# The row factors of the long sequence multiplied onto x by GpSimd, and the scale per feature put into the split of x

## The chip, the cores and the metric

The kernel runs on one core of a Trainium2 chip. The metric is the device time of one execution in microseconds (us); lower is better. Three runs of the kernel before the change took 2688.34, 2689.30 and 2693.07 us, a median of 2689.3 us.

A core has a matrix engine (TensorE, PE in the profile; loading its stationary operand is shown apart as PEld), three engines for elementwise work, which are VectorE (DVE), ScalarE (ACT) and GpSimd (POOL), and a queue that only starts DMAs (SyncE, SP). Each engine works through its own instructions strictly in order; an instruction that waits for another engine holds up all that stand behind it on its own engine.

## The reference

An encoder layer is applied to two sequences, a short one of 1024 rows (`x_prompt`) and a long one of 2048 rows (`x_sample`); 16 learned meta rows stand ahead of each. Cut to what matters here:

```python
def _rmsnorm(x, g):
    xf = x.astype(jnp.float32)
    y = xf * lax.rsqrt(jnp.mean(xf * xf, axis=-1, keepdims=True) + EPS)
    return (y * g.astype(jnp.float32)).astype(x.dtype)

def _encoder_layer(h, g_pre, w_in, b_in, ...):
    xn = _rmsnorm(h, g_pre)
    proj = xn @ w_in + b_in
    na_q, na_k, na_v, na_z, ml_qk, ml_v, ml_z, ml_o, ml_g, mg = jnp.split(proj, SPLIT_IDX, axis=-1)
    ya = neighbourhood_attention(na_q, na_k, na_v, na_rpb) * silu(na_z) @ w_a
    yb = mlstm_branch(ml_qk, ml_v, ml_g, ml_o, ...) * silu(ml_z) @ w_b
    ga, gb = jnp.split(jax.nn.sigmoid(mg), 2, axis=-1)
    return h + _rmsnorm((ga * ya + gb * yb) @ w_out, g_post)
```

The change concerns the first two lines of the layer: `xn = x * r * g_pre`, where `r` is one number per row (the inverse root of its mean square) and `g_pre` one number per feature.

## The kernel before

**The matrix products.** Operands are float32. To keep float32's precision TensorE is given each operand as a sum of a rounded part and a remainder, `x = xh + xl`, `w = wh + wl`, and every product is three matmuls: `xh*wh`, `xl*wh`, `xh*wl` (lines 217 to 219 in `mm3`, 786 to 788 in `tm_unit`). `xh` is made by ScalarE (a copy into the rounded type), `xl` by VectorE (x minus `xh`).

**Tiles and stages.** x lies transposed in SBUF, features on the 128 partitions: 1024 features are eight feature tiles k = 0 to 7, and a half of 512 rows is worked on at a time. `PLAN` is the list of column groups: `(0, 0, "m")`, `(0, 0, "nv")` for the short sequence, then `(1, 0, "mv")` and `(1, 1024, "mv")` for the two 1024-row pieces of the long one, then later groups that read x back from DRAM. `group` runs one of these: jobs of four columns, each first for the half 0 of the rows (`hf = 0`), then for half 1. Each column of a half is 24 matmuls of 128x512 (8 feature tiles times 3), and k goes up inside a column.

**Where the changed code runs.** `build_half(s, t0, res)` makes `xh` and `xl` of one half. For the long sequence (its last branch, lines 520 to 545) it runs four times: for rows 0, 512, 1024 and 1536, called builds 1 to 4 below. Each loads the rows (`tokens`), takes their squares on ScalarE and their factors on VectorE (`rsum`), spreads the factors over all partitions by a matmul with ones (`rrows`, result `rx`, one row of 512 factors on every partition), multiplies `xt` in place by `rx` and by `g_pre` (line 533, eight instructions of VectorE, one per feature tile), then splits it (line 540 ScalarE, line 541 VectorE, four of each, two feature tiles at a time). Builds 1 and 3 run beside the last job of the group before and must be done when the next group starts; builds 2 and 4 run beside `hf = 0` of their group's first job and must be done when `hf = 1` of that job starts. The halves `xh`, `xl` have two buffers each, so builds 3 and 4 also wait until TensorE has left the buffer. `xsplit` (lines 392 to 399) is the split that the short sequence uses: it takes one feature tile at a time and multiplies by the scale per feature on the way.

**What runs beside it.** The generator `sparse` issues the mLSTM scan and the neighbourhood attention between the matmuls of the dense groups. During builds 1 to 3 it is the mLSTM of the short sequence: TensorE multiplies a chunk's keys (`kth`, `ktl`, the split of the transposed keys, lines 1567 and 1568) and a chunk's scores (`sh`, `sl`, split by lines 1707 and 1713) between the columns' matmuls. Its small operands are made by ScalarE and VectorE, so these engines' work and the builds' work share two queues.

**What sets the order.** TensorE's instructions stand in the order in which the program issues them. The order on VectorE, ScalarE, GpSimd and SyncE is made by a scheduler at build time, which estimates each instruction's time; so moving a multiply from one engine to another also moves its neighbours. GpSimd's own work here is starting DMAs (lines 586, 604, 845, 677, 1107 and others) and a few memsets.

Of the kernel before, what the change touches and what calls it, by code (L numbers as in the profile page):

```python
# [10 lines left out]
F32 = mybir.dt.float32  # L11
F32R = mybir.dt.float32r
I32 = mybir.dt.int32
AF = mybir.ActivationFunctionType
ALU = mybir.AluOpType
# [122 lines left out]
class K:  # L138
# [337 lines left out]
    def build_half(self, s, t0, res):  # L476

        nc, wp = self.nc, self.wp
        if (s, t0) in self.xkept:
            assert not self.xput  # L480
            yield
            yield "scaled"
            x = []
            for name, part in zip(("xh", "xl"), self.xkept[s, t0]):
                x.append(wp.tile([P, KT, HALF], F32R, name=name, bufs=2))
                for k in range(0, KT, 4):
                    nc.sync.dma_start(x[-1][:, k:k + 4, :512].bitcast(F32), part[:, k:k + 4, :])
                yield
            res.append(tuple(x))
            return  # L490
        if s == 0:
            xts = self.xnext
            self.xnext = None
            while self.rwait:
                yield "wait"
            self.early = False
            yield "scaled"
            g = self.gpre
            p = self.psum("sm", [P, 512])
            nc.tensor.matmul(p[:, :KT], self.ident, g, start=True, stop=True)  # L500
            g = self.cp.tile([P, KT], F32, name="gx")
            nc.vector.tensor_copy(g, p[:, :KT])
            x, r = self.xparts(), []
            for e in range(4):
                self.xsplit(x, xts[e], e, 0, g)
                self.wflush(2)
                yield
            res.append(tuple(x))
            yield from self.rsum(self.toks, r)
            nc.vector.tensor_copy(self.rc[:, 4:8], r[0])  # L510
            dg = self.rdiag(r[0], self.toks[0][0])

            def rows():
                self.rrows(dg, self.rr[:, 1], "sm")
                self.xp.close()
                self.wside = self.wprep()
                self.sides.append([self.wside, 3])
            self.rwait[s, t0] = rows
        else:
            bp = self.bp  # L520
            toks, r = self.tokens(s, t0, range(4), bp, 4), []
            yield
            yield from self.rsum(toks, r)
            dg = self.rdiag(r[0], wp.tile([P, HALF], F32, name="st", bufs=4))
            xts = [self.xtload(s, t0, e, bp, 4) for e in range(4)]
            yield
            rr = bp.tile([P, 512], F32, name="rx", tag="thT", bufs=1)
            self.rrows(dg, rr, "pj")
            self.loose = False
            yield  # L530
            for k in range(KT):
                v = xts[k // 2][:, k % 2]
                nc.vector.scalar_tensor_tensor(v, v, self.gpre[:, k:k + 1], rr, op0=ALU.mult, op1=ALU.mult)
                if k % 2:
                    yield
            yield "scaled"
            x = self.xparts()
            for e in range(4):
                h = x[0][:, 2 * e:2 * e + 2, :512]
                nc.scalar.activation(h, xts[e], AF.Copy)  # L540
                nc.vector.tensor_tensor(x[1][:, 2 * e:2 * e + 2, :512], xts[e], h.bitcast(F32), op=ALU.subtract)
                yield
            res.append(tuple(x))
            self.loose = True
            self.xkeep(s, t0, x)
# [1651 lines left out]
```

## Time and profile before

| | |
|---|---|
| median of three runs | 2689.3 us |
| the profiled execution, its own time | 2690.81 us |
| the profiled execution, its span on the core | 2688.8 us |
| TensorE matmuls busy | 2641.9 us, 98% of the span |
| VectorE busy | 1942.2 us, 72% |
| ScalarE busy | 1440.3 us, 54% |
| GpSimd busy | 195.5 us, 7% |
| mean granted clock of TensorE | 0.995 |

The span is what the engines' records cover; the time measured around it is 2.0 us longer. TensorE is busy nearly all of the span, so the rows to look for are those in which it sat idle, and which engine ended that idleness. A row of the waits view reads: engine, line and tile that waited, arrow, what it waited for, then microseconds in total, times, and the longest. A row of a timeline reads: start, duration, engine, line, operation, output and inputs, and in brackets the idle time before it and what released it.

### The profile page before, as it was taken

How to read it: one execution, taken by the hardware profiler on the slowest of the kernel's cores; microseconds unless marked ns; L12 is line 12 of the kernel's file. 1: busy time of each engine (PE TensorE's matmuls, PEld its weight loads, DVE VectorE, ACT ScalarE, POOL GpSimd, SP SyncE). 2: the span in 40 equal slices, each digit the busy share in tenths (PEclk: the TensorE clock that was granted, in tenths of full speed). 3: DMA queues.
4: the chain of work that ended last, by engine and by line, in shares of the span. 5: the costliest groups of instructions: out<-in, count | busy, mean ns of one | idle time of the engine just before them, and what ended most of it. 6: DMA issues, size and time to landing. Idle time of an engine off the chain costs nothing.

```text
span 2688.8 us, 47086 instructions
## 1 busy us (share of the span) xinstructions
PE 2641.9 (98%) x15928; PEld 2331.0 (87%) x15928; DVE 1942.2 (72%) x5262; ACT 1440.3 (54%) x3388; POOL 195.5 (7%) x418
## 2 busy tenths in 40 slices
PE   9999999999999899999999999999999999999998
PEld 7898897899888899887888888887889898989888
DVE  5655678788667777546686776867478989898954
ACT  5423555554446555546665666656365656656521
POOL 0111130011301114000000000000000000000000
PEclk9999999999999999999999999999999999999999
DMA  9899988798867998989889998899899899998965
GB/s 377 323 332 338 329 288 318 269 347 304 299 222 248 364 352 295 317 270 282 261 273 337 360 301 265 277 348 324 273 324 308 257 300 286 279 310 257 327 241 202
DMA packets 394880, 805.73 MB, mean 300 GB/s; under 512 B 50608, under 2 KB 173440, under 8 KB 390800
## 3 DMA queue, kind: packets, MB, share of 16 engines
q1 hardware_dynamic: 363088, 702.49, 77.9%
q0 software_dynamic: 31552, 100.25, 10.1%
q8 instruction: 126, 2.06, 0.3%
q14 instruction: 114, 0.93, 0.1%
HBM read 548.96 MB, written 253.60 MB: 298 GB/s over the span
## 4 chain that ended last, share of the span: by engine, by line
PE 85%; DMA 8%; DVE 4%; ACT 2%; issue 1%; SPq 0%; DVEq 0%; ACTq 0%
PE pj L217 9%; PE pj L219 9%; PE pj L218 9%; PE pj L982 7%; PE pj L984 7%; PE pj L983 7%; PE pj L786 5%; PE pj L788 5%; PE pj L787 5%; PE pj L1944 3%; PE pj L1943 3%; PE pj L1945 3%; PE sm L1277 2%; DMA whl<-w 2%; PE tr L1262 2%; DMA stk<-nq 1%
## 5 line engine op out<-in xcount | busy, mean ns | idle before, releaser
L217 PE MATMUL pj<-xh,whl 128*128 128x512 f32 (+1 forms) x960 | 369.7, 385 | 2.7 <-DMA whl<-w 1.6
L219 PE MATMUL pj<-xh,whl 128*128 128x512 f32 (+1 forms) x960 | 360.9, 376 | 0.0
L218 PE MATMUL pj<-xl,whl 128*128 128x512 f32 (+1 forms) x960 | 360.2, 375 | 0.4 <-DVE xl L445 0.4
L786 PE MATMUL pj<-whl,xh 128*128 128x256 f32 (+1 forms) x1152 | 330.7, 287 | 10.5 <-DMA whl<-w 10.2
L788 PE MATMUL pj<-whl,xl 128*128 128x256 f32 (+1 forms) x1152 | 326.4, 283 | 0.0
L787 PE MATMUL pj<-whl,xh 128*128 128x256 f32 (+1 forms) x1152 | 326.1, 283 | 0.0
L786 PEld LDWEIGHTS pj<-whl,xh 128*128 128x128 f32 x1152 | 218.4, 190 | 11.5 <-DMA whl<-w 10.6
L1943 PE MATMUL pj<-whl,mh 128*128 128x256 f32 x768 | 218.3, 284 | 0.9 <-DMA whl<-w 0.9
L787 PEld LDWEIGHTS pj<-whl,xh 128*128 128x128 f32 x1152 | 218.3, 190 | 0.2
L788 PEld LDWEIGHTS pj<-whl,xl 128*128 128x128 f32 x1152 | 218.3, 189 | 0.0
L1944 PE MATMUL pj<-whl,mh 128*128 128x256 f32 x768 | 216.3, 282 | 0.0
L1945 PE MATMUL pj<-whl,mlo 128*128 128x256 f32 x768 | 215.4, 281 | 0.0
L219 PEld LDWEIGHTS pj<-xh,whl 128*128 128x128 f32 x960 | 181.2, 189 | 35.1
L217 PEld LDWEIGHTS pj<-xh,whl 128*128 128x128 f32 x960 | 181.2, 189 | 35.0 <-DMA whl<-w 2.0
L982 PE MATMUL pj<-xh,whl 128*128 128x512 f32 x512 | 206.9, 404 | 2.9 <-DMA xh<-t01h 1.5
L218 PEld LDWEIGHTS pj<-xl,whl 128*128 128x128 f32 x960 | 181.7, 189 | 30.5 <-issue 1.0
L984 PE MATMUL pj<-xh,whl 128*128 128x512 f32 x512 | 202.1, 395 | 0.0
L983 PE MATMUL pj<-xl,whl 128*128 128x512 f32 x512 | 201.0, 393 | 0.0
L1264 ACT ACTIVATE pts<-tr 96x384 fp32r<-96x384 f32 (+2 forms) x192 | 103.7, 540 | 109.2 <-PE tr L1262 108.5
L1269 DVE TENSOR_TENSOR pts<-tr,pts 96x384 fp32r<-96x384 f32 (+2 forms) x192 | 118.6, 618 | 53.5 <-ACT pts L1264 51.4
L217 PE MATMUL pj<-yh,whl 128*128 128x512 f32 x384 | 154.1, 401 | 0.0
L218 PE MATMUL pj<-yl,whl 128*128 128x512 f32 x384 | 151.5, 394 | 0.7 <-DVE yl L1845 0.7
(380 smaller groups left out, 6871.7 us busy)
## 6 DMA issues: line engine op xcount, KB each, us to landing
whl<-w SPq DMA_DIRECT2D x136, 1024.0 KB
whl<-q SPq DMA_DIRECT2D x112, 512.0 KB
w<-whl SPq DMA_DIRECT2D x36, 1024.0 KB
wraw<-wu SPq DMA_DIRECT2D x48, 512.0 KB
gt<-st SPq DMA_DIRECT2D x96, 256.0 KB
tg<-gt SPq DMA_DIRECT2D x96, 256.0 KB
q<-po POOLq DMA_DIRECT2D x26, 512.0 KB, 6.7
xt<-xt SPq DMA_DIRECT2D x24, 512.0 KB
```

The source lines that it names most:

```text
L217: mm(out, ah, bh, start=start, stop=False)
L218: mm(out, ah, bl, start=False, stop=False)
L219: mm(out, al, bh, start=False, stop=stop)
L786: nc.tensor.matmul(o, xh, wh, start=k == 0, stop=False)
L787: nc.tensor.matmul(o, xh, wl, start=False, stop=False)
L788: nc.tensor.matmul(o, xl, wh, start=False, stop=k == KT - 1)
L982: mm(bank, w[:, 0, k], xh[:, k], start=fresh and k == 0, stop=False, skip_group_check=True)
L983: mm(bank, w[:, 0, k], xl[:, k], start=False, stop=False, skip_group_check=True)
L984: mm(bank, w[:, 1, k], xh[:, k], start=False, stop=k == 3, skip_group_check=True)
L1943: nc.tensor.matmul(o, mh[:, k, xs], wh, start=clear > 0 and k == 0, stop=False)
L1944: nc.tensor.matmul(o, mh[:, k, xs], wl, start=False, stop=False)
L1945: nc.tensor.matmul(o, ml[:, k, xs], wh, start=False, stop=clear < 2 and k == KT - 1)
```

## The change

Two things change in `build_half`, in the branch for the long sequence. The eight multiplies by the row factors are now GpSimd's and no longer carry `g_pre`. The split is `xsplit`'s: eight instructions of 128x512 on ScalarE and eight on VectorE, each with `g_pre` as a scale per partition, in place of four and four of 128x1024. What is computed is the same up to rounding.

```diff
             for k in range(KT):
                 v = xts[k // 2][:, k % 2]
-                nc.vector.scalar_tensor_tensor(v, v, self.gpre[:, k:k + 1], rr, op0=ALU.mult, op1=ALU.mult)
+                nc.gpsimd.tensor_tensor(v, v, rr, op=ALU.mult)
                 if k % 2:
                     yield
             yield "scaled"
             x = self.xparts()
             for e in range(4):
-                h = x[0][:, 2 * e:2 * e + 2, :512]
-                nc.scalar.activation(h, xts[e], AF.Copy)
-                nc.vector.tensor_tensor(x[1][:, 2 * e:2 * e + 2, :512], xts[e], h.bitcast(F32), op=ALU.subtract)
+                self.xsplit(x, xts[e], e, 0, self.gpre)
                 yield
```

```python
    def xsplit(self, x, xt, e, base, gpre):
        nc = self.nc
        for k in (2 * e, 2 * e + 1):
            g, v = gpre[:, k:k + 1], xt[:, k % 2]
            h = x[0][:, k, base:base + v.shape[1]]
            nc.scalar.activation(h, v, AF.Copy, scale=g)
            nc.vector.scalar_tensor_tensor(x[1][:, k, base:base + v.shape[1]], v, g, h.bitcast(F32), op0=ALU.mult, op1=ALU.subtract)
```

Lines behind 541 stand two lower in the changed kernel: `ktl`'s line 1568 is 1566 there, `sl`'s line 1713 is 1711.

TensorE's instructions stand in the same order in both kernels. On the other engines the order changes at these places.

**GpSimd, builds 1 and 2.** `q` and `po` are DMAs of prepared weights, `raw`, `ss` and `st` small memsets for the mLSTM and the row factors. Before:

```order
L604 DMA q_4219<-po 128x1024
L604 DMA q_4221<-po 128x1024
L604 DMA q_4564<-po 128x1024
L358 MEMSET ss 128x5
L1426 MEMSET raw 128x1
L1584 MEMSET st 128x130
L1426 MEMSET raw 128x1
L604 DMA q11s_5750<-po 128x1024
```

and in the changed kernel:

```order
L602 DMA q_4219<-po 128x1024
L602 DMA q_4221<-po 128x1024
L533 ISA
L533 TENSOR_TENSOR xt<-xt,rx 128x512 x8
L602 DMA q_4564<-po 128x1024
L1424 MEMSET raw 128x1
L358 MEMSET ss 128x5
L1582 MEMSET st 128x130
L533 TENSOR_TENSOR xt<-xt,rx 128x512 x8
L1424 MEMSET raw 128x1
```

Eight multiplies stand in one piece in each build. Ahead of the first stands one instruction, ISA, that was not there before; the built program names it a reload of the library that holds GpSimd's operations.

**VectorE, build 1**, up to the second `ktl`, the remainder of the transposed keys. `vwl` and `st` belong to the mLSTM, `po` and `pr` to the prepared weights, `pj` is a column's result in PSUM. Before:

```order
L533 SCALAR_TENSOR_TENSOR xt<-xt,gpre,rx 128x512 x3
L1568 TENSOR_TENSOR ktl<-tr,kth 128x256
L533 SCALAR_TENSOR_TENSOR xt<-xt,gpre,rx 128x512 x3
L1439 SCALAR_TENSOR_TENSOR cv<-raw,cw,cv 128x16
L696 TENSOR_TENSOR pj<-pj,rr 128x512
...
L541 TENSOR_TENSOR xl<-xt,xh 128x2x512
L591 TENSOR_TENSOR pr<-pr 128x512
L1595 SCALAR_TENSOR_TENSOR st<-st,g_fb_3128,sm 128x130
L541 TENSOR_TENSOR xl<-xt,xh 128x2x512 x2
L1568 TENSOR_TENSOR ktl<-tr,kth 128x256
```

and in the changed kernel:

```order
L1566 TENSOR_TENSOR ktl<-tr,kth 128x256
L1437 SCALAR_TENSOR_TENSOR cv<-raw,cw,cv 128x16 x2
L694 TENSOR_TENSOR pj<-pj,rr 128x512
...
L1539 SCALAR_TENSOR_TENSOR vwl<-va_2774,g_wT_3114,vwh 128x130
L399 SCALAR_TENSOR_TENSOR xl<-xt,gpre,xh 128x512 x4
L694 TENSOR_TENSOR pj<-pj,rr 128x512
L399 SCALAR_TENSOR_TENSOR xl<-xt,gpre,xh 128x512 x2
L1566 TENSOR_TENSOR ktl<-tr,kth 128x256
```

No multiply stands ahead of the first `ktl` any more; ahead of the second stand six of the new split, where three of the old one stood.

**VectorE, build 2**, up to `sl`, the remainder of the second scores; `um`, `s` and `kl` belong to the mLSTM chunk. Before:

```order
L533 SCALAR_TENSOR_TENSOR xt<-xt,gpre,rx 128x512 x8
L1439 SCALAR_TENSOR_TENSOR cv<-raw,cw,cv 128x256
L541 TENSOR_TENSOR xl<-xt,xh 128x2x512 x3
...
L541 TENSOR_TENSOR xl<-xt,xh 128x2x512
L1656 TENSOR_TENSOR kl<-kf,kh 128x256
...
L1706 TENSOR_TENSOR um<-um,s_5623 128x256 x2
L1733 TENSOR_TENSOR num<-sm,num 128x128
L1713 TENSOR_TENSOR sl<-um,sh 128x256 x2
```

and in the changed kernel:

```order
L399 SCALAR_TENSOR_TENSOR xl<-xt,gpre,xh 128x512 x2
L1654 TENSOR_TENSOR kl<-kf,kh 128x256
L399 SCALAR_TENSOR_TENSOR xl<-xt,gpre,xh 128x512
L1699 TENSOR_TENSOR s_5637<-sc,s_5637 128x256
L399 SCALAR_TENSOR_TENSOR xl<-xt,gpre,xh 128x512
L1704 TENSOR_TENSOR um<-um,s_5637 128x256 x2
L1730 TENSOR_TENSOR num<-sm,num 128x260
L399 SCALAR_TENSOR_TENSOR xl<-xt,gpre,xh 128x512
L1711 TENSOR_TENSOR sl<-um,sh 128x256
L1731 TENSOR_TENSOR num<-sm,num 128x128
L1711 TENSOR_TENSOR sl<-um,sh 128x256
```

The last split of the build stood ahead of `kl`; now three splits stand between `kl` and `sl`, each waiting for ScalarE and through it for one of GpSimd's multiplies. In builds 3 and 4 GpSimd's sixteen multiplies stand in one row, ahead of the DMAs that open the neighbourhood attention (line 1107).

## The prediction

> **What bounds the kernel now.** I read the page's busy times first, then the chain that ended last, then what TensorE waited for.
>
> ```profile
> span 2688.8 us, 47086 instructions
> PE 2641.9 (98%) x15928; PEld 2331.0 (87%) x15928; DVE 1942.2 (72%) x5262; ACT 1440.3 (54%) x3388; POOL 195.5 (7%) x418
> PE 85%; DMA 8%; DVE 4%; ACT 2%; issue 1%; SPq 0%; DVEq 0%; ACTq 0%
> PE pj L786 <- DMA whl<-w: 10.2, 2, 7.6
> PE sm L219 <- DVE ktl L1568: 5.9, 5, 2.6
> ```
>
> TensorE is the bound, and its matmuls stay as they are, in number and order. So the change can move the time only through the microseconds in which TensorE stands still: it can remove some, or add some where a build's operands or the mLSTM's come later. The waits of the last row are the only ones near the builds that VectorE causes, and two of the five lie inside build 1:
>
> ```profile
> 430.97 0.38 PE L219 MATMUL sm<-vwh,ktl 128*128 128x260 f32 x1 [1.23 <-DVE ktl L1568]
> 437.32 0.28 PE L217 MATMUL sm<-vwh,kth 128*128 128x260 f32 x1
> 440.37 0.59 PE L219 MATMUL sm<-vwh,ktl 128*128 128x260 f32 x1 [2.64 <-DVE ktl L1568]
> 420.00:442.00 22.00, 18.13 (x85) 14.83 (x84) 21.19 (x52) 13.71 (x29) 0.76 (x2) 0.95 0.60 204
> 472.00:489.00 17.00, 17.00 (x83) 13.92 (x82) 14.41 (x25) 10.46 (x21) 0.10 (x1) 1.00 0.33 112
> 745.00:757.00 12.00, 12.00 (x60) 9.97 (x59) 10.21 (x41) 6.00 (x14) 0.55 (x1) 1.00 0.24 78
> 789.00:804.00 15.00, 15.00 (x68) 12.22 (x67) 14.08 (x17) 6.28 (x8) 0.00 (x0) 1.00 0.70 207
> ```
>
> The last four rows are the windows of builds 1 to 4; after the length come the busy times of PE, PEld, DVE, ACT and POOL. VectorE is full in build 1 (21.19 of 22 us) and nearly so in the others, GpSimd empty (0.00 to 0.76 us). That speaks for the move, as long as GpSimd does its part in time and does not slow VectorE.
>
> **The change part by part.** *VectorE and ScalarE.* Rows of the removed instructions, and of the same split where the kernel already uses it:
>
> ```profile
> L533 DVE SCALAR_TENSOR_TENSOR xt<-xt,gpre,rx x32: 717/748/754, 425.7 to 795.2; 128x512 f32<-128x512 f32 x32
> L541 DVE TENSOR_TENSOR xl<-xt,xh x16: 1218/1225/1229, 435.6 to 801.5; 128x1024 fp32r<-128x1024 f32 x16
> L540 ACT ACTIVATE xh<-xt x16: 1044/1050/1067, 433.1 to 798.7; 128x1024 fp32r<-128x1024 f32 x16
> L399 DVE SCALAR_TENSOR_TENSOR xl<-xt,gx,xh x8: 742/746/751, 32.4 to 37.4; 128x512 fp32r<-128x512 f32 x8
> L398 ACT ACTIVATE xh<-xt,gx x8: 727/732/741, 31.6 to 35.9; 128x512 fp32r<-128x512 f32 x8
> ```
>
> Per build VectorE loses 8 x 0.748 + 4 x 1.225 = 10.9 us and gains 8 x 0.746 = 6.0: 4.9 us less. ScalarE gets 8 x 0.732 - 4 x 1.050 = 1.7 us more, covered by its idle 8.3 us of 22 in build 1.
>
> *GpSimd's multiply, p.* The trace has no two-operand instruction of GpSimd. Its nearest rows:
>
> ```profile
> L1584 POOL MEMSET st<- 128x130 f32 x8 | 1.7, 210 | 97.0 <-DVE ccl L1685 92.3 <-DMA raw<-mq 4.7
> L358 POOL MEMSET ss<- 128x5 f32 x6 | 0.6, 103 | 76.0 <-DVE nwt L165 76.0
> L728 POOL COPY km<-st 128x16 f32<-128x16 f32 x4 | 0.9, 228 | 0.0
> ```
>
> The memsets give (210 - 103) / 125 = 0.86 ns per element on a fixed 0.10 us. One pass over 512 elements is 0.54 us, the floor; two passes (one per operand, the write beside them) are 0.98, three 1.42. The copy, if all of its 228 ns above 0.10 were per element, would give 8 ns each and 4.2 us, the ceiling; 16 elements are mostly fixed cost, so I stay with the memsets' slope and take 1.2, midway between two passes and three.
>
> *Spacing, q.* Whether GpSimd's two-operand instruction runs beside one of VectorE's with two operands in SBUF, the trace cannot show, since GpSimd has none. Ends: q = p = 1.2, they do not disturb each other; or they take turns, and each multiply is followed by one split, q = 1.2 + 0.75 = 1.95. I take turns as the likelier: both read the same memory at the same time, VectorE's queue is full in these windows, and nothing in the rows shows two such streams at once. The Trainium skill, page "SBUF — State Buffer", section "Who interferes with whom", says that VectorE with two SBUF inputs and a GpSimd instruction that reads SBUF exclude each other for a whole instruction; no run here shows it so far, and by it the sum would be the one below, without it that of the first rival.
>
> *The reload ahead of the first multiply.* Its place is behind the two DMA starts at 419.06 (over at 420.23). Nothing in the trace prices it: at least nothing, at most GpSimd's slowest transfer under this load, 10.7 us; I take the other row, 6.7 us, so that the first multiply starts at 426.9.
>
> ```profile
> 419.06 1.17 POOL L604 DMA_DIRECT2D q<-po  x2 [12.38 <-DVE st L378]
> q<-po POOLq DMA_DIRECT2D x26, 512.0 KB, 6.7
> pr<-wu POOLq DMA_DIRECT2D x16, 512.0 KB, 10.7
> ```
>
> The Trainium skill, page "GPSIMD Engine Reference", section "2.1 Instruction dispatch", puts the first call into freshly loaded code at about 6 us; this estimate would bring the start 0.7 us forward.
>
> *Build 1.* The first `ktl` no longer has multiplies ahead of it, so the wait of 1.23 goes. The second stands behind six splits: sixth multiply done at 426.9 + 6q, then ScalarE 0.73, VectorE 0.75 and `ktl` itself 0.42, 1.9 in all.
>
> ```profile
> 439.90 0.42 DVE L1568 TENSOR_TENSOR ktl<-tr,kth 128x256 fp32r<-128x256 f32 x1
> 462.87 0.50 PE L217 MATMUL pj<-xh,whl 128*128 128x512 f32 x1 [1.61 <-DMA whl<-w]
> ```
>
> Taking turns: 426.9 + 11.7 + 1.9 = 440.5, against 440.37 now: **+0.1**, the wait of 1.23 given back in a longer second one. The whole build has time until the group starts at 462.87, so its own result is not late.
>
> *Build 2.* The factors are ready at 473.44; TensorE wants `sl` at 488.45.
>
> ```profile
> 472.84 0.60 ACT L385 ACTIVATE rx<-pj 128x512 f32<-128x512 f32 x1 [0.49 <-PE pj L384]
> 486.36 0.76 DVE L1713 TENSOR_TENSOR sl<-um,sh 128x256 fp32r<-128x256 f32 x2
> 488.45 0.28 PE L219 MATMUL sm<-v,sl 128*128 128x130 f32 x1
> ```
>
> Now `sl` ends at 487.1, 1.3 us early. In the new order it follows the eighth split: 473.44 + 8q + 0.73 + 0.75, and 1.0 for the two `sl` and `num` between them. With q = 1.95 that is 491.5: **+3.0**. Queued behind these splits on VectorE are `um`, `num`, `sl`, on ScalarE `sh` and a column's evacuation; the first to be missed is `sl`.
>
> *Build 3.* The multiplies start at 745.67 and no split waits for the last of them, as ScalarE makes `xh` behind the evacuation at 753.64 anyway. But GpSimd works beside the mLSTM's chain on VectorE:
>
> ```profile
> 745.08 0.59 ACT L385 ACTIVATE rx<-pj 128x512 f32<-128x512 f32 x1
> 753.64 0.69 ACT L708 ACTIVATE st<-pj,bfm 128x512 f32<-128x512 f32 x1 [0.68 <-PE pj L219]
> 751.69 0.76 DVE L1706 TENSOR_TENSOR um<-um,s 128x256 f32<-128x256 f32 x2
> 753.05 0.42 DVE L1713 TENSOR_TENSOR sl<-um,sh 128x256 fp32r<-128x256 f32 x1
> 753.97 0.28 PE L219 MATMUL sm<-v,sl 128*128 128x130 f32 x1
> ```
>
> Taking turns, the two `um` and two `sl`, each with both inputs in SBUF, wait for one multiply each: 4 x 1.2 = 4.8, less the 0.5 between the end of `sl` and TensorE's wish: **+4.3**. Without disturbance 0: VectorE has 1.4 us less ahead of them.
>
> *Build 4.* Start 789.85 (ScalarE's `rx` at 789.25), no mLSTM beside it. TensorE takes feature tile k = 7 from 808.25 (the row is the first of its three matmuls in build 4's first column):
>
> ```profile
> 789.25 0.60 ACT L385 ACTIVATE rx<-pj 128x512 f32<-128x512 f32 x1 [2.37 <-PE pj L384]
> 808.25 0.40 PE L217 MATMUL pj<-xh,whl 128*128 128x512 f32 x1
> 751.08 0.55 POOL L1107 DMA_DIRECT2D qB<-onehot  x1 [22.41 <-PE sc L1694]
> 772.87 1.02 POOL L1194 DMA_DIRECT2D kx<-masks  x2
> 824.36 0.29 PE L1231 MATMUL sc<-kx,qB 128*128 128x288 f32 x1
> DMA to landing us min/median/max: 7.0/7.6/8.2
> ```
>
> Taking turns, the eighth split ends at 789.85 + 15.6 + 1.5 = 806.9: **0**, with 1.3 to spare. GpSimd's DMAs that open the attention stand behind these multiplies and move from 751 to 773 to about 806; their first use is the matmul at 824.36, and the masks' landing takes 8.2 us at most (last row), so that is covered.
>
> *Sum:* 0.1 + 3.0 + 4.3 + 0 = +7.4 us on the profiled execution's 2690.8, or 2698.2; its time lies 1.5 above the median of the runs, so the forecast is **2697 us** as a median (2689.3 + 7.4 = 2696.7). With p = 0.98 the builds give -1.2, +1.3, +3.4, 0: +3.5; with p = 1.42 they give +1.4, +4.8, +5.2 and +0.4: +11.8. A reload of 10.7 adds up to 4.0. Own range 2692 to 2704.
>
> **The rivals.** *No disturbance* (the engines run side by side, q = 1.2). Build 1's sixth multiply is done at 434.1, `ktl` at 436.0, when TensorE arrives (437.32 less the 1.23); both waits shrink, though the chain of ScalarE ahead of `kth` keeps about 0.9: -3.0. Builds 2 to 4 meet their times (485.5 for `sl`, against 488.45). 2689.3 - 3.0 = 2686 us, within 0.2%: not slower. For it: GpSimd is idle and VectorE gets 4.9 us back per build. Against it: it needs two engines to stream 512 elements from two operands each without one delaying the other.
>
> *A dear multiply* (p of 4.2 as the copy row could mean, decisive from about 2.1, where build 4's last tile passes 808.25). Then, even without turns, build 1 gives 426.9 + 25.2 + 1.9 - 440.4 = +13.6, build 2 473.4 + 33.6 + 2.5 - 488.4 = +21.1, build 4 789.85 + 33.6 + 1.5 - 808.25 = +16.7, together 51: 2740 us. The slope of the memsets speaks against it.
>
> *Luck of the order.* The scheduler also swaps loads on SP further on; TensorE's wait of 7.6 us for a weight load (first block) is of that kind. If it vanished in addition to build 1's two waits: 2689.3 - 3.0 - 7.6 = 2679 us. Nothing in the order says that it does.
>
> **How the numbers follow.** Taking turns 0.55, no disturbance 0.30, dear multiply 0.07, luck 0.08. 0.2% is 5.4 us, about what a measurement of this kernel tells from no change, so the borders are 2683.9 and 2694.7. A sixth of the first case (p near two passes) falls inside them: 0.09. Slower 0.46 + 0.07 = 0.53, same 0.30 + 0.09 = 0.39, faster 0.08. The range must hold both middle cases, of both signs: 2685 to 2706; the likeliest's own is the 2692 to 2704 above.
>
> **What would show it.** Right: multiplies of GpSimd of 1.0 to 1.4 us start to start alone, nearer 2 beside VectorE; VectorE's `um` and `sl` longer or later in build 3; a wait of TensorE for `sl` or `sh` of about 3 us near 488 and of about 4 near 754. Wrong: multiplies at an even 1.2 with VectorE's rows unchanged, no idle TensorE in builds 2 and 3, and one or none for `ktl` near 440. A first multiply later than 431 would mean a dearer reload; a wait in a column's matmuls near 808 a dearer multiply.

## The result, and the profile after

The changed kernel takes **2706.6 us** in the median of four runs (2702.6 to 2710.8), the kernel before 2691.2 (2688.3 to 2694.0): **1.0056 times as long, 95% interval 1.0045 to 1.0068**, about 15 us slower. The forecast was 2697 us, with a range of 2685 to 2706. The profiled execution took 2710.75 us, 1.8 of them around its span of 2709.0; it is the slowest of the four, so a time read from it is a few us too long for the median.

The page after, its span and busy times:

```profile
span 2709.0 us, 47121 instructions
PE 2652.7 (98%) x15928; PEld 2340.1 (86%) x15928; DVE 1950.8 (72%) x5246; ACT 1444.2 (53%) x3404; POOL 241.5 (9%) x450
```

TensorE has the same 15928 matmuls, yet it is *busy* 10.8 us longer (2641.9 before). VectorE has 16 instructions fewer and should be 20 us less busy; it is 8.6 us busier. Two things have become longer that the change does not touch. The first shows in VectorE's timeline in build 1. A row has the start, the duration and the instruction. In the kernel before:

```profile
421.12 0.16 DVE L166 SCALAR_TENSOR_TENSOR nwy<-nwt,nwy 128x4 f32<-128x4 f32 x1
422.31 0.16 DVE L166 SCALAR_TENSOR_TENSOR nwy<-nwt,nwy 128x4 f32<-128x4 f32 x1
423.65 1.11 DVE L1819 TENSOR_SCALAR hb<-hb,mv,nwy 128x128 f32<-128x128 f32 x4
```

and in the changed kernel, beside GpSimd's eight multiplies, which run from 420.78 to 430.80 (beyond line 540 its line numbers are two lower):

```profile
420.76 0.15 DVE L165 TENSOR_TENSOR nwt<-nwt,mv 128x4 f32<-128x4 f32 x1
420.95 1.15 DVE L166 SCALAR_TENSOR_TENSOR nwy<-nwt,nwy 128x4 f32<-128x4 f32 x1
422.14 1.22 DVE L164 SCALAR_TENSOR_TENSOR nwt<-nwy 128x4 f32<-128x4 f32 x1
...
428.38 1.22 DVE L166 SCALAR_TENSOR_TENSOR nwy<-nwt,nwy 128x4 f32<-128x4 f32 x1
429.52 0.69 DVE L694 TENSOR_TENSOR pj<-pj,rr 128x512 f32<-128x512 f32 x1
```

These are the steps of the inverse root (`rsqrt8`), 4 elements in each partition. The last one ahead of GpSimd's start takes 0.15 us; the next seven take 1.15 to 1.22 us each where they took 0.16, one multiply of GpSimd apiece. The instruction at 429.52, with one operand in PSUM, has its normal duration although a multiply runs beside it. GpSimd's own line, and that of the new splits (least, median and longest duration in ns):

```profile
L533 POOL TENSOR_TENSOR xt<-xt,rx x32: 1262/1340/2267, 420.8 to 813.9; 128x512 f32<-128x512 f32 x32
L399 DVE SCALAR_TENSOR_TENSOR xl<-xt,gpre,xh x40: 719/744/1784, 5.7 to 819.2; 128x512 fp32r<-128x512 f32 x40
```

The three waits of TensorE in build 1 that follow, and the later ones:

```profile
432.47 0.39 PE L217 MATMUL sm<-vwh,kth 128*128 128x260 f32 x1 [3.15 <-DVE vwl L1539]
434.55 0.59 PE L219 MATMUL sm<-vwh,ktl 128*128 128x260 f32 x1 [1.58 <-DVE ktl L1566]
446.26 0.39 PE L219 MATMUL sm<-vwh,ktl 128*128 128x260 f32 x1 [2.20 <-DVE ktl L1566]
...
777.82 0.39 PE L218 MATMUL tr<-ccl,q 128*128 128x260 f32 x1 [1.93 <-DVE ccl L1683]
902.78 0.59 PE L784 MATMUL pj<-whl,xh 128*128 128x264 f32 x1 [7.68 <-DMA whl<-w]
967.32 0.39 PE L784 MATMUL pj<-whl,xh 128*128 128x256 f32 x1 [2.79 <-DMA whl<-w]
1028.40 0.58 PE L784 MATMUL pj<-whl,xh 128*128 128x256 f32 x1 [4.24 <-DMA whl<-w]
1165.50 0.77 PE L980 MATMUL pj<-xh,whl 128*128 128x512 f32 x1 [3.31 <-DMA xh<-t01h]
```

The row near 778 belongs to build 3, the last four are waits beyond the builds. Before, the weight waits there were two, and that for `t01h` was 1.47 us:

```profile
889.74 0.59 PE L786 MATMUL pj<-whl,xh 128*128 128x264 f32 x1 [7.60 <-DMA whl<-w]
981.51 0.39 PE L786 MATMUL pj<-whl,xh 128*128 128x256 f32 x1 [2.59 <-DMA whl<-w]
```

The second is TensorE's busy time. The next view has windows of the changed kernel behind the first wait; the columns after the length are the busy times of PE, PEld, DVE, ACT and POOL, then the granted clock.

```profile
430.00:432.00 2.00, 0.00 (x0) 0.00 (x0) 2.00 (x7) 1.70 (x4) 0.80 (x1) 1.00 0.00 0
432.00:434.00 2.00, 0.50 (x2) 0.30 (x2) 2.00 (x7) 0.73 (x3) 0.00 (x0) 0.94 0.06 20
434.00:436.00 2.00, 1.45 (x5) 1.37 (x6) 1.77 (x6) 1.05 (x5) 0.00 (x0) 0.50 0.55 192
436.00:438.00 2.00, 2.00 (x6) 1.54 (x5) 1.80 (x5) 2.00 (x6) 0.60 (x1) 0.50 0.30 92
438.00:440.00 2.00, 2.00 (x7) 1.56 (x6) 1.19 (x3) 2.00 (x5) 0.00 (x0) 0.50 0.58 234
440.00:442.00 2.00, 2.00 (x9) 1.64 (x8) 2.00 (x6) 2.00 (x5) 0.00 (x0) 0.85 0.34 131
```

From 433.8 to 440.6 us the granted clock is 0.50. Behind the matmul at 434.55 TensorE is busy there without a pause, but it starts a matmul of 128x512 only every 0.43 us, and every 0.23 us again from 440.7 on: the wait has a tail that no row calls a wait. Adding up every pause in TensorE's rows, and half of the half-clock time in which it worked, accounts for the whole time. In profiled executions (us, the pauses and the loss summed from all matmul rows and clock records of the trace; "rest" is the time to the last matmul less both):

| kernel | span | pauses | lost at half clock | rest |
|---|---|---|---|---|
| before | 2688.8 | 38.0 | 8.5 | 2633.6 |
| before, once more | 2691.4 | 40.0 | 10.4 | 2632.4 |
| changed | 2709.0 | 47.9 | 19.8 | 2633.0 |
| changed, once more | 2703.3 | 48.3 | 14.0 | 2632.6 |
| finer split, multiplies on VectorE | 2695.8 | 44.6 | 12.7 | 2630.2 |

The rest is the same within 0.13%: the change does nothing but add pauses (9.1 us in the mean of the two pairs) and half-clock time (7.5 us).

### The profile page after: what moved, and what is told of

Same layout as the page of the kernel before. It is cut to its first block, busy times and chain, and to the rows that moved or that the text cites. A ratio compares the mean times of both kernels' runs of the same rounds, so it can differ in the third digit from the quotient of the medians.

```text
span 2709.0 us, 47121 instructions
## 1 busy us (share of the span) xinstructions
PE 2652.7 (98%) x15928; PEld 2340.1 (86%) x15928; DVE 1950.8 (72%) x5246; ACT 1444.2 (53%) x3404; POOL 241.5 (9%) x450
## 3 DMA queue, kind: packets, MB, share of 16 engines
q8 instruction: 126, 2.06, 0.3%
## 4 chain that ended last, share of the span: by engine, by line
PE 83%; DMA 8%; DVE 6%; ACT 2%; issue 1%; SPq 0%; DVEq 0%; ACTq 0%
PE pj L217 9%; PE pj L219 9%; PE pj L218 9%; PE pj L980 7%; PE pj L982 7%; PE pj L981 7%; PE pj L784 4%; PE pj L786 4%; PE pj L785 4%; PE pj L1942 3%; PE pj L1941 3%; PE pj L1943 3%; DMA whl<-w 3%; PE sm L1275 3%; PE tr L1260 2%
## 5 line engine op out<-in xcount | busy, mean ns | idle before, releaser
L784 PEld LDWEIGHTS pj<-whl,xh 128*128 128x128 f32 x1152 | 220.2, 191 | 16.3 <-DMA whl<-w 15.8
```

What stands on the lines that cost most here:

```text
L784: nc.tensor.matmul(o, xh, wh, start=k == 0, stop=False)
```

## The experiments

Theory A: GpSimd's multiply and a VectorE instruction of certain forms take turns, and the pauses this gives TensorE are followed by half clock. Its rivals: B, the waits beyond 880 us are chance; C, the finer split and the scheduler's other order cost, GpSimd does not; D and E, on the weight waits, stand with their runs.

**The changed kernel once more** (`after_again`), the same kernel.

> The changed kernel once more, unchanged, so that its waits are seen twice. Theory A (taking turns, with the clock behind it: beside a GpSimd multiply each VectorE instruction with two inputs in SBUF takes one multiply's 1.2 us, and a TensorE pause of 2 us or more is followed by a stretch of 3.4 to 10 us at half clock): 2703 to 2710 us; the seven short instructions L164 to L166 from 421 us take 1.15 to 1.22 us each again, the waits near 432, 434 and 446 us come again within 0.3 us, and the span less the time lost at half clock stays within 2 us of the first run's 2681.9. Theory B (the loss beyond 900 us is chance of the DMA): the waits of 4.24 us near 1028 and 3.31 us near 1165 do not come again, and the time falls to 2697 to 2702.

2703.5 us (2698.7 to 2705.8), ratio 1.0040 [1.0028, 1.0053]. The seven short instructions take 1.15 to 1.22 us again, and build 1's waits come again: 3.16, 1.58 and 2.72 (the last 0.5 longer than in the first profile). The weight waits come again too, 8.69, 4.03 and 2.85 (near 1028), 15.6 in all against 14.7; the one for `t01h` is 0.93 in place of 3.31. Theory B falls for the weights and holds for `t01h`. The half-clock loss moves from 19.8 to 14.0 us between two executions of one program.

**The kernel before once more** (`before_again`), the same kernel.

> The kernel before, unchanged, so that its own waits are seen twice. If the waits are those of its order: 2689 to 2694 us, waits of 1.2 and 2.6 us in build 1, 7.6 for a weight load near 890, 2.6 near 981, and none for a weight load near 1005 to 1015. If the waits beyond 880 us are chance: their sum (10.2 for the loads) differs by 3 us or more, and one near 1015 can come here too.

2691.5 us, ratio 0.9996 [0.9987, 1.0006]. Build 1's waits 1.23 and 2.64; weights 8.20 and 3.13 (11.3 in all), none near 1015. So the third weight wait belongs to the change and not to chance; it stands in every profile of a kernel with the finer split and the scheduler's order of DMAs, and in none of the three profiles of the kernel before and its variant below.

**Finer split alone** (`split_only`):

```
-                nc.gpsimd.tensor_tensor(v, v, rr, op=ALU.mult)
+                nc.vector.tensor_tensor(v, v, rr, op=ALU.mult)
```

> The scale per feature goes into the split as in the change, but the eight multiplies of a build stay on VectorE (two inputs). Theory A (turns and clock): nothing runs on GpSimd beside VectorE, the short instructions L164 to L166 take 0.16 us again, build 1 has no TensorE wait above 2.7 us, VectorE loses 4.9 us per build: 2683 to 2691 us. Theory C (the finer split, 32 instructions in place of 16 per engine, and the other order of loads on SP make the loss): 2698 us or more, with the long waits for weights near 900 and 1028 us still there.

2697.5 us, ratio 1.0024 [1.0013, 1.0036]: between both expectations. The 4.9 us per build were wrong in that text: they count the multiplies, which stay here, so VectorE has 8 x 0.684 + 8 x 0.747 = 11.4 us per build against 10.9. Without GpSimd the waits for `vwl` and `ccl` are gone; what stays is a second `ktl` behind six finer splits and three weight waits:

```profile
432.45 0.39 PE L219 MATMUL sm<-vwh,ktl 128*128 128x260 f32 x1 [0.94 <-DVE ktl L1566]
443.44 0.39 PE L219 MATMUL sm<-vwh,ktl 128*128 128x260 f32 x1 [4.23 <-DVE ktl L1566]
893.40 0.59 PE L784 MATMUL pj<-whl,xh 128*128 128x264 f32 x1 [7.81 <-DMA whl<-w]
957.79 0.39 PE L784 MATMUL pj<-whl,xh 128*128 128x256 f32 x1 [2.86 <-DMA whl<-w]
1017.88 0.58 PE L784 MATMUL pj<-whl,xh 128*128 128x256 f32 x1 [3.25 <-DMA whl<-w]
```

So a part of C is right: the loss is not GpSimd's alone.

**GpSimd in builds 2 to 4** (`gp_builds234`) **and in build 1 alone** (`gp_build1`): `(nc.gpsimd if t0 else nc.vector)`, and the reverse.

> As the change, but in build 1 the multiplies stay on VectorE; GpSimd multiplies in builds 2 to 4. Theory A: build 1's part goes (5.9 us by the matmul behind the second ktl: 2.3 of wait, the rest half clock), what hangs on builds 3 and 4 stays: 2697 to 2702 us. Theory A with everything behind build 1 hanging on its shift: 2689 to 2693. Theory C (split and order): no change against the changed kernel, 2704 to 2709.

> The other half: GpSimd multiplies in build 1 alone, VectorE in builds 2 to 4. Theory A: build 1 costs its 5.9 us, the waits for ccl near 778 us and for t01h near 1165 go, and with VectorE's 4.9 us back in the other builds the time is 2692 to 2698 us. Theory C: 2704 to 2709. If builds 2 to 4 were what costs, and build 1 nothing: 2685 to 2690.

2702.5 us [1.0026, 1.0050] and 2702.9 us [1.0023, 1.0050]. The waits go where theory A puts them: `vwl` 3.14 near 432 only with GpSimd in build 1, `ccl` 1.94 near 772 only with GpSimd in the others. The times do not tell the builds apart: each half costs some 5 us over `split_only`, both together 6 to 9, and the intervals of the halves overlap with that of `split_only`. The weight waits beyond 880 us differ more than these times, 19.3 us with GpSimd in builds 2 to 4 and 13.2 with GpSimd in build 1. The second expectation (2692 to 2698) is missed in the median, though the profiled execution of that kernel has a span of 2694.6. In build 1 itself TensorE waits 6.9 us in the changed kernel and 5.2 in `split_only`, with 10.2 and 3.4 us at half clock, so there the tail grew more than the waits. How the loss divides over the builds stays open.

**The pairs by themselves** (`side_by_side`), a kernel of its own:

> None of the reference's work; a table of pairs by itself. Five VectorE instructions of one form (two inputs in SBUF, one input in SBUF, one in PSUM and one in SBUF; 128x4 and 128x512) run beside an idle GpSimd, beside memsets (write only), copies (one input) and multiplies (two inputs) of 128x512 on GpSimd. Turns at each instruction (theory A): the 128x4 form with two SBUF inputs takes 0.16 us beside an idle GpSimd and 1.1 to 1.3 beside multiplies, 0.5 to 1.2 beside copies, 0.16 beside memsets; the 128x512 form with two SBUF inputs grows by the same 1.0 to 1.2 us; the forms with one SBUF input stay as they are in all four. Shared bandwidth (rival): the 128x512 forms grow by a factor, the 128x4 ones hardly, and the forms with one SBUF input grow too.

Its groups, shapes kept apart; the tile's name tells VectorE's operands (SS two in SBUF, S one in SBUF, PS one in PSUM and one in SBUF) and what GpSimd did (idle, none = memset, one = copy, two = multiply); behind the bar the busy time and the mean ns of one:

```profile
L49 DVE SCALAR_TENSOR_TENSOR vSS_beside_idle<-y,b 128x512 f32<-128x512 f32 x5 | 3.5, 692 | 8.9 <-SPq L31 8.8
L49 DVE SCALAR_TENSOR_TENSOR vSS_beside_none<-y,b 128x512 f32<-128x512 f32 x5 | 3.5, 692 | 0.2
L49 DVE SCALAR_TENSOR_TENSOR vSS_beside_one<-y,b 128x512 f32<-128x512 f32 x5 | 4.3, 861 | 6.0 <-SPq L31 5.9
L49 DVE SCALAR_TENSOR_TENSOR vSS_beside_two<-y,b 128x512 f32<-128x512 f32 x5 | 6.3, 1254 | 2.1 <-SPq L31 2.0
...
L51 DVE TENSOR_SCALAR vS_beside_idle<-y 128x512 f32<-128x512 f32 x5 | 2.1, 426 | 0.2
L51 DVE TENSOR_SCALAR vS_beside_none<-y 128x512 f32<-128x512 f32 x5 | 3.2, 632 | 6.0 <-SPq L31 5.9
L51 DVE TENSOR_SCALAR vS_beside_two<-y 128x512 f32<-128x512 f32 x5 | 4.9, 989 | 5.3 <-SPq L31 5.2
...
L53 DVE TENSOR_TENSOR vPS_beside_two<-ps,y 128x512 f32<-128x512 f32 x5 | 3.4, 688 | 5.3 <-SPq L31 5.2
L53 DVE TENSOR_TENSOR vPS_beside_two<-ps,y 128x4 f32<-128x4 f32 x5 | 0.8, 159 | 6.9 <-SPq L31 6.8
```

With two SBUF operands VectorE waits for a GpSimd instruction that reads SBUF (692 to 861 and 1254) and not for one that only writes (692). The means also hold instructions that were not held; the three held by multiplies took 1.63 us each, and a pair came every 1.67 us, less than 1.26 for the multiply and 0.69 for VectorE's instruction one behind the other. With one operand in PSUM nothing waits for a multiply at either size (688, 159), so it is not shared bandwidth. One point of the expectation falls: the `tensor_scalar` with a single SBUF operand is stretched as well, even by memsets (426 to 632). The four short SS instructions beside multiplies took 2.77 us together, less than one turn each. Singly they took 1.23, 0.16, 1.11 and 0.16: every second one began in the 0.08 us between two multiplies, and such a gap does not stand between the kernel's multiplies. That the gap is the reason was not tried by itself.

The Trainium skill, page "SBUF — State Buffer", section "Who interferes with whom", says that VectorE with two SBUF inputs excludes a GpSimd instruction that reads SBUF, and that `tensor_scalar` can contend in a two-port mode. The first agrees with these rows (1254 and 861 beside reads, 692 beside writes); the held `tensor_scalar` fits the second, but no run here shows in which mode it ran.

**Write only, in the kernel** (`memset_twice`):

```
-                nc.gpsimd.tensor_tensor(v, v, rr, op=ALU.mult)
+                nc.gpsimd.tensor_copy(v[:, :1], rr[:, :1])
+                nc.gpsimd.memset(v, 1.0)
+                nc.gpsimd.memset(v, 1.0)
```

> The changed kernel with each GpSimd multiply replaced by a copy of one column and two memsets of the same 128x512 elements, about as long together, and at the same place in GpSimd's queue; x is left out of the result, which is constant. Theory A (turns come from GpSimd reading SBUF): the seven short instructions from 421 us take 0.16 us, except where one meets the one-column copy (0.3 at most), no wait for ccl near 778, and the time is split_only's within 4 us, 2694 to 2701. Rival (GpSimd's queue and its late results cost, however they are made): 2703 to 2709, with the wait for vwl of 3 us near 432 and for ccl of 1.9 near 778 still there.

2701.2 us [1.0024, 1.0046]. VectorE's timeline beside the memsets of build 1 (line numbers here as in the kernel before):

```profile
422.05 0.16 DVE L164 SCALAR_TENSOR_TENSOR nwt<-nwy 128x4 f32<-128x4 f32 x1
422.24 0.16 DVE L165 TENSOR_TENSOR nwt<-nwt,mv 128x4 f32<-128x4 f32 x1
422.44 0.16 DVE L166 SCALAR_TENSOR_TENSOR nwy<-nwt,nwy 128x4 f32<-128x4 f32 x1
423.14 0.70 DVE L696 TENSOR_TENSOR pj<-pj,rr 128x512 f32<-128x512 f32 x1 [0.54 <-PE pj L219]
423.75 5.94 DVE L1819 TENSOR_SCALAR hb<-hb,mv,nwy 128x128 f32<-128x128 f32 x2
```

The short instructions are back at 0.16 us (one of 0.20), so they were held by GpSimd's reads; the wait for `vwl` is gone, and that for `ccl` falls from 1.93 to 0.34. But the single-operand `tensor_scalar` behind them, 1.11 us for four in the kernel before, takes 5.94 for the first two, until the row of memsets is over: the form that `side_by_side` found to be held by memsets too. So one victim took the place of another. The time lies some 4 us above `split_only`'s, with intervals that overlap, at the upper edge of what theory A gave and below the rival's. How much of GpSimd's cost is turns alone, this run does not separate.

**TensorE's pauses by themselves** (`pe_pauses`), bursts of matmuls with pauses between:

> None of the reference's work; bursts of 60 to 75 matmuls of 128x512 with pauses of about 1 to 6 us between them, nine lengths, six of each. Theory A (the clock is judged in fixed stretches of 3.4 us): half clock comes in multiples of 3.4 us on one grid; after pauses below about 1.7 us never, after pauses above 5 us always, and between them sometimes, by where the pause lies in the grid. Rival (a threshold on the pause alone): one length below which it never and above which it always comes.

Half clock came after 0 of 6 pauses of 1.7 us, 5 of 6 of 2.3, 4 of 6 of 3.0, 4 of 6 of 3.6, and after all of 4.3 to 7.2. That 2.3 us could hit and 3.6 us miss rules out a threshold on the pause alone. All stretches begin on one grid of 3.413 us. Sorted by how long TensorE stood still within one step of the grid (counted from the matmul rows and clock records; left this kernel, right the twelve profiled executions of the others):

```
step at full clock, pause in it   next step at half     next step at half
      below 1.6 us                    0 of 218             0 of 9221
      1.6 to 1.9                      0 of 9               5 of 19
      1.9 to 2.0                      0 of 1               8 of 8
      above 2.0                      36 of 36             59 of 59
step at half clock, pause in it
      below 0.3 us                    0 of 31              1 of 73
      0.3 to 0.6                      0 of 5               2 of 4
      above 0.6                      22 of 22             35 of 35
```

A step with more than 2.0 us of pause always made the next one half, one with less than 1.6 never, and 13 of the 37 between did; a half step led back to full in 110 of 113 cases with less than 0.6 us of pause, and in none of 57 with more. So a pause of 2 to 4 us costs nothing, about 1.7 or about 3.4 us on top, by where it lies. The wait for `kth` near 690 shows it: 2.06 us before, without a half step; 2.18 in the changed kernel, with two.

The Trainium skill, page "TensorE: Matmul & The Clock Gate", section "What's actually happening", has the free-running window of 3413 ns, which agrees; its table gives an idle window of about 3.4 us as the condition, where here about 2 us inside one step were enough.

**One weight load put back** (`after_early_load`). In the new order SP issues the second load of weight w13 behind ten transfers that stood after it before. Here they stand behind it again (`add_manual_dep`, order only).

> The changed kernel with one load of SP put back: the second load of weight w13, which the scheduler moved behind ten other transfers, is issued ahead of the attention's operands again, as before the change. Theory D (this order makes the new wait for a weight load near 1028 us): the weight waits behind 960 us fall from 7.0 us (2.79 + 4.24) to about 2.6 to 3, the half clock near 1021 goes with them, and the time falls by 4 to 7 us against the changed kernel, to 2698 to 2702. Theory E (the transfers are simply late because the builds were): no gain, 2703 to 2708.

2704.3 us [1.0031, 1.0059]: no gain. The weight waits are 8.77, 1.07 and 6.49, 16.3 in all; the wait moved and did not shrink. That load by itself is not the cause.

**SP's whole order put back**, in the changed kernel (`after_sp_order`) and in the finer split (`split_sp_order`); 78 of 1964 transfers stand elsewhere than in the scheduler's own order of the changed kernel:

```
+        for a, b in zip(SP_ORDER, SP_ORDER[1:]):
+            tc.add_manual_dep(sp[b], sp[a].name, ...)
```

> The changed kernel with the whole order of SP's transfers put back to that of the kernel before (all 1964 transfers, where 78 stood in another place). Theory D (the scheduler's other order of SP makes the later weight waits): the waits for weight loads between 890 and 1040 us fall from 14.7 us to 10 to 11.5, the half-clock stretches behind them from 17 us to about 10, and the time by 4 to 7 us against the changed kernel. Theory E (not the order: the transfers of this stage run at the limit of the DMA engines, and any shift of the work beside them makes them late): no gain, 2703 to 2708 us.

> The finer split with the multiplies on VectorE (split_only), and SP's order as before the change. Theory D: weight waits of 10 to 11.5 us, 2690 to 2693 us. Theory E: as split_only, 2695 to 2699, weight waits of 13 to 15 us. In both, no wait for ccl near 778 us, and the short instructions of VectorE at 0.16 us.

2700.7 us, 1.0032 [1.0019, 1.0044], and 2693.5 us, 1.0009 [1.0000, 1.0018]. With the runs above this makes a table of two by two (medians; the changed kernel's two medians in one cell). The first column has each kernel's own order as the scheduler made it; the two differ from each other in at least 28 places, so the second column, with one order for both, is the cleaner measure of GpSimd:

| | scheduler's order of SP | order before |
|---|---|---|
| finer split, multiplies on VectorE | 2697.5 | 2693.5 |
| finer split, multiplies on GpSimd | 2703.5 and 2706.6 | 2700.7 |

GpSimd costs 6 to 9 us in the first column and 7.2 in the second, the order 4.0 in the upper row and 2.8 to 5.9 in the lower; the finer split alone 2.0 over the 2691.5 of the kernel before, which its interval hardly tells from nothing. By the ratios to the kernel before that ran beside each, GpSimd costs 4 to 9 and 6 us, the order 4 and 2 to 6. The intervals of neighbours in a row still overlap a little, so the order's share is likely rather than sure. The waits of `after_sp_order`, then of `split_sp_order`:

```profile
904.10 0.59 PE L784 MATMUL pj<-whl,xh 128*128 128x264 f32 x1 [8.10 <-DMA whl<-w]
1053.67 0.39 PE L784 MATMUL pj<-whl,xh 128*128 128x256 f32 x1 [1.01 <-DMA whl<-w]
```

```profile
890.35 0.59 PE L784 MATMUL pj<-whl,xh 128*128 128x264 f32 x1 [7.53 <-DMA whl<-w]
980.70 0.38 PE L784 MATMUL pj<-whl,xh 128*128 128x256 f32 x1 [0.97 <-DMA whl<-w]
1014.42 0.58 PE L784 MATMUL pj<-whl,xh 128*128 128x256 f32 x1 [4.88 <-DMA whl<-w]
```

In the first the weight waits fall from 14.7 to 9.1 as theory D has it, in the second only from 13.9 to 13.4. The time moves as D says, the waits bear it out in one profile of two, and in that one a wait for a weight load near 467 grows to 2.9 us (0.85 in the changed kernel): why the loads come late is not settled.

**A try at something faster than both** (`before_ktl_first`): the kernel before, with the multiplies and splits that stood ahead of the two awaited `ktl` of build 1 queued behind them.

> The kernel before, with five instructions of VectorE in build 1 set behind the ktl that TensorE waits for: the third to fifth multiply behind the first ktl, two of the splits behind the second; SP's order as before. Theory A: the waits of 1.23 and 2.64 us near 431 and 440 shrink to 0 to 0.9 each and no half-clock stretch follows them: 2.5 to 4.5 us less than the kernel before, 2686.5 to 2689. Theory E (what is won ahead of 500 us is waited for again at the weight loads beyond 880): those waits grow from 10 to 11 us to 13 or more, and the time stays at 2690 to 2693.

2689.5 us, ratio 1.0002 [0.9990, 1.0013]: the same time. Of the two `ktl` waits one is gone and the other is down to 0.84 us, as theory A has it, but its gain did not come. Theory E's reason did not hold either: the weight waits beyond 880 us are 10.8 us in all, much as before. Two other waits took their place:

```profile
438.90 0.36 PE L217 MATMUL sm<-vwh,kth 128*128 128x260 f32 x1 [2.79 <-DVE st L1595]
465.46 0.79 PE L217 MATMUL pj<-xh,whl 128*128 128x512 f32 x1 [4.47 <-DMA whl<-w]
```

No version tried is faster than the kernel before.

## Why the forecast was too low, step by step

*That TensorE's order stays and only its pauses can move the time.* The first half is right. The second is **the step that failed**: "the change can move the time only through the microseconds in which TensorE stands still". The rest of 2630 to 2634 us in every kernel shows what was missing, the half clock behind the pauses. Over all runs the time net of half clock (span times granted clock, nine runs of the changed kernel and eleven of `before_again`) rises from 2674.9 to 2683.4, **+8.5 us against the +7.4 forecast**, and the half-clock loss from 14.7 to 19.2, +4.5 us (+7.5 in the profiled executions of the table), which no term of the sum held. The rows of before had shown it: the window from 420 to 442 has a clock of 0.95 behind the wait of 2.64.

*Taking turns* was the right mechanism, and GpSimd's price was well sized: 1.26 us at least and 1.34 in the median against 1.2 taken. The reload cost nothing that the trace shows (factors at 420.70, first multiply at 420.78), against 6.7 taken; of the about 6 us that the prediction cites beside it nothing shows either. But in build 1 the turns were sought at the wrong instructions. The forecast let GpSimd alternate with the splits, which come later there. GpSimd begins as soon as its factors are there, at 420.78, where VectorE before had reached its first multiply at 425.7; so it fell on the seven steps of `rsqrt8`, and 7 x 0.16 us became 7 x 1.2. The spacing q of the multiplies was 10.02 / 8 = 1.25 us there, and 1.55 in build 2 (12.41 / 8), against 1.95. In builds 2 and 4 multiplies and splits do alternate, a pair in 1.70 us and a split of up to 1.78 us: two instructions in turn took less than the sum of their durations, which the forecast had added up.

*Build 1, +0.1.* Waits of 1.23, 2.64 and 1.61 became 3.15, 1.58, 2.20 and 0.85: +2.3, and three half steps (5.1 us of loss at most) in place of one (1.7). The matmul behind the second `ktl` comes 5.9 us later (440.37 to 446.26).

*Builds 2 and 3, +3.0 and +4.3.* There is no wait for `sl` or `sh`. What failed here is who waits: the forecast paired each `sl` with the next matmul that reads the name. Each kernel has 96 `sl` and 96 matmuls of line 219 that read one; taken in order, the `sl` of 486.36 in the kernel before is read at 498.17, 11.4 us after it is made, and that of 753.05 at 772.06. In the changed kernel build 2's `sl` is made at 495.53 and still 7.6 us early. The rows after show a pair made at 746.38, the next at 767.61, and TensorE taking two in between without a pause:

```profile
746.38 0.82 DVE L1711 TENSOR_TENSOR sl<-um,sh 128x256 fp32r<-128x256 f32 x2 [0.15 <-ACT sh L1705]
767.61 0.42 DVE L1711 TENSOR_TENSOR sl<-um,sh 128x256 fp32r<-128x256 f32 x1
```

```profile
763.14 0.28 PE L219 MATMUL sm<-v,sl 128*128 128x130 f32 x1
768.24 0.27 PE L219 MATMUL sm<-v,sl 128*128 128x130 f32 x1
```

So neither is the pair of 767.61; that one is first read behind `ccl`'s matmul of 777.82, some 10 us after it is made. Slack of that size had been read as 1.3 and 0.5 us. What build 3 does cost is the 1.93 for `ccl` near 778, made behind the chain that the turns had held up: in place of +4.3.

*Build 4, 0:* right, and with its margin: the eighth split ends at 819.94, 1.2 us ahead of TensorE's matmul at 821.18 (1.3 forecast), and no wait follows.

*Beyond the builds* the sum had no term, only a rival with the opposite sign, luck of the order. The weight waits rose from 10.2 to 14.7 us (11.3 to 15.6 in the second pair), about +4.4. The two-by-two table puts 2 to 6 us on SP's order; how is open.

*The rivals.* No disturbance falls by the seven rows, a dear multiply by its 1.3 us. That the time net of half clock came out at +8.5, near +7.4, is a coincidence of terms: builds 2 and 3 were put too high, build 1 and the stretch beyond the builds too low.

## What to carry to other kernels

Before work moves to GpSimd, list every VectorE instruction that will stand beside it, the shortest first, and look at where its operands lie: with two in SBUF each of them can cost a whole GpSimd instruction, with one in PSUM none did, and a `tensor_scalar` was held with even one in SBUF. Count pauses of TensorE twice: one of 2 to 4 us can cost up to 3.4 us more at half clock, and the busy time of an engine whose work is unchanged tells it. When a change lets a scheduler order again, put the old order of the DMA queue under the new kernel and measure, so that the two effects stand apart; and match each operand to its reader by its buffer, not by its name.

## What the runs showed of the hardware that was not expected

- The half clock comes in steps of 3.413 us on one grid; a step with about 2 us of pause is enough to make the next one half, and in a half step more than 0.6 us keeps it so.
- One program differs in half-clock loss from execution to execution (19.8 and 14.0 us in two profiles of the changed kernel), and so in its time.
- A `tensor_scalar` with one f32 operand in SBUF is held by GpSimd's memsets (426 to 632 ns, and 5.94 us for two of 128x128 in the kernel), where instructions with two operands are not.
